# The second round of a fused down projection: each weight sum emitted one unit earlier, and the residual additions spread over more pairs

## Chip, core and metric

The kernel runs on one core of one Trainium2 chip. The metric is device time in microseconds (us) for one execution of the whole program. Five engines work side by side, each on its own in-order list of instructions: TensorE does the matrix products (PE in the profile; PEld is its weight load), VectorE (DVE) and ScalarE (ACT) do elementwise work, GpSimd (POOL) does elementwise work on the side, and SyncE (SP) issues the DMA transfers. [...]

## The reference

A decoder block of sequence 512 and width 1024, in float32. The change touches only the last product, the down projection of the feed-forward part, and the final norm that follows it:

```python
def reference(x, norm_mix_g, w_in, ..., w_ffn_gate, w_ffn_up, w_ffn_down, norm_final_g):
    ...
        h = h + jnp.einsum('bsd,de->bse', merged, w_out[layer])
        u = rmsnorm(h, norm_ffn_g[layer])
        z = (jax.nn.silu(jnp.einsum('bsd,df->bsf', u, w_ffn_gate[layer]))
             * jnp.einsum('bsd,df->bsf', u, w_ffn_up[layer]))
        h = h + jnp.einsum('bsf,fd->bsd', z, w_ffn_down[layer])
    return rmsnorm(h, norm_final_g)
```

`z` is 512x2816 and `w_ffn_down` 2816x1024, so the weight has 22 rows of blocks of 128.

## The kernel before

**High and low parts.** Every product is made of three TensorE products on a faster number format. An operand is split into a high part (a rounded copy) and a low part (what the rounding left): high*high, high*low and low*high are added in PSUM. For a weight, `Weights.split` does this: ScalarE writes the high part `wh` (line 118), then VectorE writes the low part `wl` as weight minus `wh` (line 122). So each weight passes SyncE (load into a tile `raw`), ScalarE, VectorE and TensorE in turn. A unit is one `raw` tile of 128x2048, a quarter of it per product tile; it is split in two halves, the "granules". Names carry the numbers: `raw74` is a unit, `wh149` and `wl149` the parts of its second granule.

**The down projection** is computed by a scheme of fewer block products (as Strassen's): 2x2 blocks of `z` and of the weight are combined by sums and differences, and seven products take the place of eight. It runs in two rounds. The first round uses sums of weight blocks (kind `r1` in `Weights.sums`) and runs between the gate and up projections. The second round, which the change is about, goes over the 11 pairs of weight rows (kind `r2`, units 74 to 84): the even row of a pair needs the sum of its two halves, which VectorE writes in place into the `raw` tile (line 130, `raw<-raw`) before ScalarE can make the high part. A pair gives four products, each 2 row tiles times 3 matmuls of 128x512: `a11b11` and `n1y1` from the even granule, then `a12b21` and `n4b22` from the odd one, 24 matmuls in all. In the profile the PSUM tiles show as `a11b`, `s3y`, `a22y` and `s2y` (the last three are banks taken over from the first round).

**Order.** From the last up projection on, the instructions of VectorE, ScalarE and TensorE keep the order in which the code emits them (`manual_schedule`, the part called `by_hand`). `W.get` hands out the next granule and first splits up to two granules beyond it. `wh` and `wl` have three buffers each, `raw` has two in the old pool and, once the memory of the up projection's input is free, two more (`W.more`). Before the loop over the pairs there is an entry in which the last first-round products, the combination of the last pair's `z` (tile `z8`, lines 1018 to 1029) and the split of unit 74 (`b11h`, `b11l`, `wh149`, `y1h`, `y1l`) interleave. Inside the loop VectorE also adds the first-round products into the residual `hn`, in lump form: four additions behind pair 1, four behind pair 2, and behind pair 3 the last combination of `z` with its split (`zh`, `zl`, lines 1084 to 1086) and the load of the norm's gains. The last three pairs (the tail, units 82 to 84, granules 164 to 169 in the order 164, 166, 165, 167, 168, 169) are split ahead and used by `tail`, product by product, so that finished row tiles can be normalized while others are still multiplied. After `by_hand.close()` the order is a scheduler's.

## Time and profile before

| | |
|---|---|
| median of 3 runs | 903.86 us (902.82 to 904.28) |
| the profiled execution | 904.07 us, span 902.3 us, granted TensorE clock 0.996 |
| busy TensorE | 886.7 us, 98% of the span |
| busy VectorE, ScalarE, GpSimd | 551.4, 396.8 and 154.8 us |
| second round and tail | 827.5 to 894.7 us of the span |

The span is the time from the first to the last instruction that the profiler saw; the execution's own time lies 1.8 us above it. In a timeline row the columns are the start, the length, the engine, the line, the operation, out<-in, the shape and the count; in brackets stands how long the engine had been idle and what ended that. TensorE's matmuls overlap: each row is about 0.39 us long, but at full clock one starts every 0.227 us, so time is counted from start to start. The row of a stretch gives each engine's busy time, then the granted clock of TensorE (1.00 is full), the DMA engines' share and GB/s.

### The profile page before, as it was taken

Reading aid. Unit: us, or ns where it says so; the run is one execution under the profiler, and the core shown is the slowest. Engines: PE = TensorE matmul, PEld = TensorE weight load, DVE = VectorE, ACT = ScalarE, POOL = GpSimd, SP = SyncE. Lnnn points to the kernel's source line nnn. Section 1 sums busy time; section 2 is a strip of 40 time slices with the busy share of each in tenths; the row PEclk is TensorE's granted clock in tenths of the full one; section 3 lists DMA queues with packets and bytes.
Section 4 is the critical chain, followed back from the end, with each engine's and each line's share of the span. In section 5 each row is a group of like instructions: output and inputs, shape, how many; then the busy total and the mean of one; then the engine's idle time right before and its main releaser. Section 6 shows DMA issues by size and latency. Waiting matters only on the chain.

```text
span 902.3 us, 11245 instructions
## 1 busy us (share of the span) xinstructions
PE 886.7 (98%) x4410; PEld 748.0 (83%) x4410; DVE 551.4 (61%) x838; ACT 396.8 (44%) x637; POOL 154.8 (17%) x150
## 2 busy tenths in 40 slices
PE   8999999999999999999999999999999999999986
PEld 7988889888898988888888887888888888887775
DVE  5577877647484755745445345666666556666765
ACT  6566775645363545315333333333333233333444
POOL 3004434300000000000000003332122333320006
PEclk9999999999999999999999999999999999999998
DMA  7231311222212141221434222443434424336522
GB/s 259 94 94 47 94 48 47 94 94 94 94 55 86 48 141 47 94 94 48 140 105 175 61 83 91 139 134 100 140 96 138 139 96 140 125 109 232 208 97 94
DMA packets 74642, 97.26 MB, mean 108 GB/s; under 512 B 2042, under 2 KB 64604, under 8 KB 74588
## 3 DMA queue, kind: packets, MB, share of 16 engines
q1 hardware_dynamic: 74428, 96.27, 32.6%
q8 instruction: 35, 0.57, 0.3%
q10 hardware_dynamic: 160, 0.27, 0.1%
q14 instruction: 19, 0.16, 0.1%
HBM read 94.43 MB, written 2.10 MB: 107 GB/s over the span
## 4 chain that ended last, share of the span: by engine, by line
PE 91%; DVE 3%; ACT 2%; SPq 1%; issue 1%; POOL 0%; DMA 0%; DVEq 0%; POOLq 0%; ACTq 0%
PE ps_big L396 13%; PE ps_big L398 13%; PE ps_big L397 13%; PE ps_f L397 9%; PE ps_f L398 9%; PE ps_f L396 9%; PE s3y L981 2%; PE s2y L981 2%; PE a22y L981 2%; PE ps_v L413 2%; PE ps_v L414 2%; PE ps_v L412 2%; PE ps_o L413 2%; PE ps_o L414 2%; PE ps_o L412 2%; PE pv L538 1%
## 5 line engine op out<-in xcount | busy, mean ns | idle before, releaser
L118 ACT ACTIVATE wh<-raw 128x1024 fp32r<-128x1024 f32 (+1 forms) x168 | 172.1, 1031 | 352.6 <-PE ps_f L397 137.5
L122 DVE TENSOR_TENSOR wl<-raw,wh 128x1024 fp32r<-128x1024 f32 (+1 forms) x168 | 208.4, 1246 | 120.6 <-ACT wh L118 120.4
L396 PE MATMUL ps_big<-uh,wh 128*128 128x512 f32 x376 | 148.8, 396 | 0.0
L397 PE MATMUL ps_big<-ul,wh 128*128 128x512 f32 x376 | 147.8, 393 | 0.0
L398 PE MATMUL ps_big<-uh,wl 128*128 128x512 f32 x376 | 147.7, 393 | 0.0
L397 PE MATMUL ps_f<-u2l,wh 128*128 128x512 f32 x352 | 137.4, 390 | 0.0
L396 PE MATMUL ps_f<-u2h,wh 128*128 128x512 f32 x352 | 137.0, 390 | 0.2 <-ACT u2h L163 0.2
L398 PE MATMUL ps_f<-u2h,wl 128*128 128x512 f32 x352 | 137.0, 389 | 0.0
L398 PEld LDWEIGHTS ps_big<-uh,wl 128*128 128x128 f32 x376 | 70.7, 188 | 14.1
L397 PEld LDWEIGHTS ps_big<-ul,wh 128*128 128x128 f32 x376 | 70.8, 188 | 13.6
L396 PEld LDWEIGHTS ps_big<-uh,wh 128*128 128x128 f32 x376 | 70.7, 188 | 13.5
L396 PEld LDWEIGHTS ps_f<-u2h,wh 128*128 128x128 f32 x352 | 66.0, 188 | 14.2 <-ACT u2h L163 0.5
L398 PEld LDWEIGHTS ps_f<-u2h,wl 128*128 128x128 f32 x352 | 66.1, 188 | 13.9 <-issue 0.2
L397 PEld LDWEIGHTS ps_f<-u2l,wh 128*128 128x128 f32 x352 | 66.1, 188 | 13.7 <-issue 0.2
L946 POOL TENSOR_TENSOR zg<-zg,sgf 128x512 f32<-128x512 f32 x22 | 39.5, 1797 | 190.8 <-ACT sgf L168 190.8
L292 POOL TENSOR_TENSOR r<-ss,neghalf 128x4 f32<-128x4 f32 x8 | 10.1, 1260 | 232.8 <-DVE ss L291 232.8
L130 DVE TENSOR_TENSOR raw<-raw 128x512 f32<-128x512 f32 x44 | 31.9, 724 | 28.6 <-DMA raw<-in_w_ffn_down_dram 28.3
L943 DVE TENSOR_TENSOR zg<-ps_f,R 128x512 f32<-128x512 f32 x22 | 15.1, 691 | 37.9 <-PE ps_f L398 37.9
L947 POOL TENSOR_TENSOR zg<-zg,R 128x512 f32<-128x512 f32 x22 | 37.0, 1683 | 1.7
L412 PE MATMUL ps_v<-wh,uh 128*128 128x256 f32 x128 | 36.5, 285 | 0.0
L413 PE MATMUL ps_v<-wl,uh 128*128 128x256 f32 x128 | 36.3, 284 | 0.0
L414 PE MATMUL ps_v<-wh,ul 128*128 128x256 f32 x128 | 36.2, 284 | 0.0
(328 smaller groups left out, 1615.4 us busy)
## 6 DMA issues: line engine op xcount, KB each, us to landing
raw<-in_w_in_dram SPq DMA_DIRECT2D x27, 1024.0 KB, 5.1
raw<-in_w_ffn_gate_dram SPq DMA_DIRECT2D x11, 1024.0 KB, 5.1
raw<-in_w_ffn_up_dram SPq DMA_DIRECT2D x11, 1024.0 KB, 5.2
raw<-in_w_ffn_down_dram SPq DMA_DIRECT2D x11, 1024.0 KB, 4.8
raw<-in_w_ffn_down_dram SPq DMA_DIRECT2D x22, 512.0 KB, 4.6
raw<-in_w_branch_attn_dram SPq DMA_DIRECT2D x4, 1024.0 KB, 5.5
raw<-in_w_branch_hgrn_dram SPq DMA_DIRECT2D x4, 1024.0 KB, 4.8
raw<-in_w_out_dram SPq DMA_DIRECT2D x4, 1024.0 KB, 5.3
```

The costliest lines, as they stand in the source:

```text
L118: nc.scalar.activation(hv, src, AF.Copy)
L122: (low or nc.vector).tensor_tensor(lv, src, hv.bitcast(F32), ALU.subtract)
L130: add = lambda o, i0, i1: self.nc.vector.tensor_tensor(o, i0, i1, ALU.add)
L396: pe.matmul(ps, wh[:, k, :], ah[:, k, :], start=k == 0, stop=False)
L397: pe.matmul(ps, wh[:, k, :], al[:, k, :], start=False, stop=False)
L398: return raw_ins(pe.matmul(ps, wl[:, k, :], ah[:, k, :], start=False, stop=k == KD - 1))
L412: pe.matmul(ps, ah[:, k0 + k, ts], wh[:, k, :], start=first and k == 0, stop=False)
L413: pe.matmul(ps, ah[:, k0 + k, ts], wl[:, k, :], start=False, stop=False)
L414: pe.matmul(ps, al[:, k0 + k, ts], wh[:, k, :], start=False, stop=last and k == nk - 1)
L946: pool_e.tensor_tensor(zg, zg, sg, ALU.mult)
L947: pool_e.tensor_tensor(zg, zg, R, ALU.mult)
L981: pe.matmul(ps[i], x[:, ts], w, start=first and n == 0, stop=last and n == 2)
```

## The change

Two things. First, the sum of a unit's even row leaves its own split: `sums_ahead` maps a granule to a later granule, and the split of the first emits the sum of the later one between its high and its low part. The map sends each granule of the second round to the one two further on, so the sum of unit u+1 stands ahead of the low part of unit u's even granule; odd rows have no sum, and `summed` keeps any sum from being made twice. The same holds in the tail, and the last sums of the first round (unit 73) move up in the same way. Second, the eight residual additions are spread two per pair over pairs 1 to 4, and the last combination of `z` moves from pair 3 to pair 5 with the release of its pool and the load of the gains.

```diff
@@ split
         if kind in ("r1", "r2"):
-            self.sums(u, half, raw)
+            self.sums(i)
...
             high.tensor_copy(hv, src)
+        if i in self.sums_ahead:
+            self.sums(self.sums_ahead[i])
         with low_after or nullcontext():
             (low or nc.vector).tensor_tensor(lv, src, hv.bitcast(F32), ALU.subtract)
...
-    def sums(self, u, half, raw):
-
-        kind, _, rows = self.units[u]
-        x = [raw[:, 512 * i:512 * i + 512] for i in range(4)]
+    def sums(self, i):
+
+        if i in self.summed or i >= len(self.grans):
+            return
+        self.summed.add(i)
+        u, kind, half = self.grans[i]
+        _, _, rows = self.units[u]
+        x = [self.raw[u][:, 512 * n:512 * n + 512] for n in range(4)]
@@ block_kernel
     r0 = len(W.grans) - NF
+    W.sums_ahead = {r0 - 2: r0 - 1}
...
-    W.sums(W.grans[r0][0], 0, raw)
+    made = list(range(r0 + 1, stream_end + 1))
+    made += [stream_end + 1 + g for g in (0, 2, 1, 3, 4, 5)]
+    W.sums_ahead.update(zip(made[1:], made[3:]))
+    W.sums(r0)
     W.split(r0 + 1)
...
-        if p == 1:
-            for i in range(2):
-                onto(i, 1, s2c[i])
-                tt(evs[i], s2c[i], evs[i], ALU.add)
-        if p == 2:
-            for i in range(2):
-                onto(2 + i, 1, evs[i])
-                onto(2 + i, 0, evs[i], ALU.subtract)
-        if p == 3:
+        if p in (1, 2):
+            onto(p - 1, 1, s2c[p - 1])
+            tt(evs[p - 1], s2c[p - 1], evs[p - 1], ALU.add)
+        if p in (3, 4):
+            onto(p - 1, 1, evs[p - 3])
+            onto(p - 1, 0, evs[p - 3], ALU.subtract)
+        if p == 5:
             tt(n4, a12, s2, ALU.subtract)
             split_form(zh[:, NP - 1], zl[:, NP - 1], z8[:, 0:4, :])
             fp.release()
...
-    for g in (0, 2, 1, 3, 4, 5):
-        if g < 2:
-            W.split(stream_end + 1 + g)
+    for g in made[-2 * TAIL_P:]:
+        if g < stream_end + 3:
+            W.split(g)
         else:
-            W.split(stream_end + 1 + g, wd, 4)
+            W.split(g, wd, 4)
```

TensorE and GpSimd keep their order throughout. On SyncE unit 75 is loaded ahead of unit 76 (it was the other way round), and the load of the gains (`gfin`) moves from between units 82 and 83 to behind unit 84. Three places show what moves on VectorE and ScalarE; the lines after the change lie 2 to 10 further down.

The entry, on VectorE, where the last first-round sums (`raw73`) and the combination of the last `z` stand. Before:

```order
L122 TENSOR_TENSOR wl145_6592<-raw72_6511,wh145_6591 128x1024
L122 TENSOR_TENSOR wl146_6623<-raw73_6585,wh146_6622 128x512
L1018 TENSOR_TENSOR z8_6615<-ps_f_6626,zg_6510 128x2x256
L1019 TENSOR_TENSOR z8_6615<-z8_6615 128x256
L975 TENSOR_TENSOR f1l_6617<-z8_6615,f1h_6616 128x256
L130 TENSOR_TENSOR raw73_6585<-raw73_6585 128x512 x2
L122 TENSOR_TENSOR wl147_6658<-raw73_6585,wh147_6657 128x1024
L975 TENSOR_TENSOR b11l_6687<-raw74_6618,b11h_6686 128x512
L1026 TENSOR_TENSOR z8_6615<-ps_f_6661,zg_6548 128x2x256
```

The same place on VectorE, changed:

```order
L126 TENSOR_TENSOR wl145_6592<-raw72_6511,wh145_6591 128x1024
L138 TENSOR_TENSOR raw73_6585<-raw73_6585 128x512 x2
L126 TENSOR_TENSOR wl146_6623<-raw73_6585,wh146_6622 128x512
L1027 TENSOR_TENSOR z8_6615<-ps_f_6628,zg_6510 128x2x256
L1028 TENSOR_TENSOR z8_6615<-z8_6615 128x256
L983 TENSOR_TENSOR f1l_6617<-z8_6615,f1h_6616 128x256
L126 TENSOR_TENSOR wl147_6658<-raw73_6585,wh147_6657 128x1024
L983 TENSOR_TENSOR b11l_6687<-raw74_6618,b11h_6686 128x512
L1035 TENSOR_TENSOR z8_6615<-ps_f_6661,zg_6548 128x2x256
```

The two sums of unit 73 move from behind the first combination of `z` to ahead of it, past `wl146`.

The loop, on VectorE, from the low parts of unit 76 (pair 2) on. `s2c`, `z8` and `ev` hold first-round products. Before:

```order
L122 TENSOR_TENSOR wl152_6789<-raw76_6734,wh152_6788 128x1024
L122 TENSOR_TENSOR wl153_6805<-raw76_6734,wh153_6804 128x1024
L1048 TENSOR_TENSOR hn_4420<-hn_4420,s2c_6751 128x512
L1078 TENSOR_TENSOR ev_6701<-s2c_6751,ev_6701 128x512
L1048 TENSOR_TENSOR hn_4420<-hn_4420,z8_6615 128x512
L1078 TENSOR_TENSOR ev_6702<-z8_6615,ev_6702 128x512
L130 TENSOR_TENSOR raw77_6737<-raw77_6737 128x512
L122 TENSOR_TENSOR wl154_6829<-raw77_6737,wh154_6828 128x1024
L122 TENSOR_TENSOR wl155_6845<-raw77_6737,wh155_6844 128x1024
L1048 TENSOR_TENSOR hn_4420<-hn_4420,ev_6701 128x512 x2
L1048 TENSOR_TENSOR hn_4420<-hn_4420,ev_6702 128x512 x2
L130 TENSOR_TENSOR raw78_6754<-raw78_6754 128x512
```

The same place on VectorE, changed:

```order
L126 TENSOR_TENSOR wl152_6789<-raw76_6734,wh152_6788 128x1024
L126 TENSOR_TENSOR wl153_6806<-raw76_6734,wh153_6805 128x1024
L1057 TENSOR_TENSOR hn_4420<-hn_4420,s2c_6751 128x512
L1089 TENSOR_TENSOR ev_6701<-s2c_6751,ev_6701 128x512
L138 TENSOR_TENSOR raw78_6754<-raw78_6754 128x512
L126 TENSOR_TENSOR wl154_6827<-raw77_6737,wh154_6826 128x1024
L126 TENSOR_TENSOR wl155_6844<-raw77_6737,wh155_6843 128x1024
L1057 TENSOR_TENSOR hn_4420<-hn_4420,z8_6615 128x512
L1089 TENSOR_TENSOR ev_6702<-z8_6615,ev_6702 128x512
L138 TENSOR_TENSOR raw79_6785<-raw79_6785 128x512
L126 TENSOR_TENSOR wl156_6865<-raw78_6754,wh156_6864 128x1024
L126 TENSOR_TENSOR wl157_6882<-raw78_6754,wh157_6881 128x1024
```

Ahead of a unit's low parts now stands the sum of the next unit, and two additions instead of four lie between units.

The tail, on VectorE, from the last granule of unit 81 on. Before:

```order
L122 TENSOR_TENSOR wl163_7005<-raw81_6864,wh163_7004 128x1024
L130 TENSOR_TENSOR raw82_6912<-raw82_6912 128x512
L122 TENSOR_TENSOR wl164_7046<-raw82_6912,wh164_7045 128x1024
L130 TENSOR_TENSOR raw83_6948<-raw83_6948 128x512
L122 TENSOR_TENSOR wl166_7051<-raw83_6948,wh166_7050 128x1024
L130 TENSOR_TENSOR raw82_6912<-raw82_6912 128x512
L122 TENSOR_TENSOR wl165_7056<-raw82_6912,wh165_7055 128x1024
L122 TENSOR_TENSOR wl167_7060<-raw83_6948,wh167_7059 128x1024
```

The same place on VectorE, changed (the first sum of `raw82` and that of `raw83` now stand further up, ahead of `wl162` and of `wl163`):

```order
L126 TENSOR_TENSOR wl163_7006<-raw81_6861,wh163_7005 128x1024
L138 TENSOR_TENSOR raw82_6899<-raw82_6899 128x512
L126 TENSOR_TENSOR wl164_7047<-raw82_6899,wh164_7046 128x1024
L126 TENSOR_TENSOR wl166_7052<-raw83_6937,wh166_7051 128x1024
L126 TENSOR_TENSOR wl165_7056<-raw82_6899,wh165_7055 128x1024
L126 TENSOR_TENSOR wl167_7060<-raw83_6937,wh167_7059 128x1024
```

No sum is left between the low parts of granules 164, 166 and 165.

At the very end of the tail, on ScalarE, where the last squares for the norm (`jkd`) and the scaling of the last row tiles (`hn`) stand. Before:

```order
L163 ACTIVATE jkd_7186,s2d_7081<-hn_4420 128x512
L163 ACTIVATE jkd_7208,s2d_7104<-hn_4420 128x512
L163 ACTIVATE jkd_7220,s2d_7104<-hn_4420 128x256
L163 ACTIVATE jkd_7223,s2d_7104<-hn_4420 128x256
L163 ACTIVATE hn_4420<-hn_4420,r1d_7192 128x512
L163 ACTIVATE hn_4420<-hn_4420,r1d_7229 128x512
```

The same place on ScalarE, changed:

```order
L171 ACTIVATE jkd_7186,s2d_7081<-hn_4420 128x512
L171 ACTIVATE jkd_7208,s2d_7104<-hn_4420 128x512
L171 ACTIVATE jkd_7220,s2d_7104<-hn_4420 128x256
L171 ACTIVATE hn_4420<-hn_4420,r1d_7192 128x512
L171 ACTIVATE jkd_7223,s2d_7104<-hn_4420 128x256
L171 ACTIVATE hn_4420<-hn_4420,r1d_7229 128x512
```

The scaling of row tile 0 (`r1d_7192`) now stands between the two last squares of row tile 1. The code of this part is not edited; the scheduler chose this order.

## Prediction

> **What bounds the kernel now.** I read the page's busy shares first (TensorE 98%), then who made TensorE wait in the second round and tail, then its timeline around each wait. The list of waits from 780 us on names four places (engine, waiting line, releaser, total, times, longest):

> ```profile
> PE a11b L981 <- DVE wl L122: 1.5, 2, 0.8
> PE a11b L1109 <- ACT wh L118: 1.5, 1, 1.5
> PE a11b L1109 <- DVE wl L122: 0.8, 1, 0.8
> PE s3y L981 <- DVE y1l L975: 0.5, 1, 0.5
> ```

> That is 4.3 us of waits, but they cost more, as the starts of the matmuls show:

> ```profile
> 827.49 0.40 PE L981 MATMUL s2y<-wh,f1l 128*128 128x512 f32 x1
> ...
> 829.04 0.50 PE L981 MATMUL s3y<-y1l,zh 128*128 128x512 f32 x1 [0.51 <-DVE y1l L975]
> ...
> 830.31 0.39 PE L981 MATMUL a22y<-wh,zh 128*128 128x512 f32 x1
> ...
> 849.47 0.42 PE L981 MATMUL a11b<-wh,zh 128*128 128x512 f32 x1
> ...
> 856.30 0.50 PE L981 MATMUL a11b<-wh,zh 128*128 128x512 f32 x1
> ...
> 862.89 0.39 PE L981 MATMUL a11b<-wh,zh 128*128 128x512 f32 x1
> ...
> 873.77 0.39 PE L1109 MATMUL a11b<-wh,zh 128*128 128x512 f32 x1
> ...
> 876.11 0.50 PE L1109 MATMUL a11b<-wh,zh 128*128 128x512 f32 x1 [1.49 <-ACT wh L118]
> 877.36 0.67 PE L1109 MATMUL a11b<-wl,zh 128*128 128x512 f32 x1 [0.76 <-DVE wl L122]
> ...
> 881.11 0.39 PE L1109 MATMUL a11b<-wl,zh 128*128 128x512 f32 x1
> ...
> 894.30 0.39 PE L1109 MATMUL s2y<-wh,zl 128*128 128x512 f32 x1
> ```

> 862.89 and 873.77 are the first matmuls of unit 80 and of the tail, two units or 48 matmuls apart: 10.88 / 48 = 0.2267 us each, with no wait. By this rate each stretch has a loss:
> - 827.49 to 830.31, 7 matmuls: 2.82 against 1.59, loss 1.23.
> - 830.31 to 849.47, 84 matmuls: 19.16 against 19.04, loss 0.12.
> - 849.47 to 862.89 (units 78 and 79), 48 matmuls: 13.42 against 10.88, loss 2.54.
> - 873.77 to 894.30, 71 matmuls: 20.53 against 16.10, loss 4.43.

> Together 8.3 us is what an unbroken TensorE would save. In the last term sits a slow stretch behind the two waits:

> ```profile
> 877.36:881.11 3.75, 3.75 (x9) 2.94 (x10) 3.75 (x4) 2.13 (x3) 0.66 (x1) 0.54 0.00 0
> ```

> The granted clock is 0.54 there; 9 matmuls took 3.75 instead of 2.04, so 1.7 of the 4.43 is clock, the other 2.7 the waits.

> **The change part by part.** It adds and removes no instruction; it moves 11 VectorE sums, 8 additions, one combination with its split, and two loads.

> *The loop, the 2.54.* Before, VectorE and ScalarE took turns, shown by two units of VectorE and one of ScalarE:

> ```profile
> 840.78 0.69 DVE L130 TENSOR_TENSOR raw<-raw 128x512 f32<-128x512 f32 x1
> 842.74 2.36 DVE L122 TENSOR_TENSOR wl<-raw,wh 128x1024 fp32r<-128x1024 f32 x2 [1.26 <-ACT wh L118]
> 845.01 2.49 DVE L1048 TENSOR_TENSOR hn<-hn,ev 128x512 f32<-128x512 f32 x4
> 847.42 0.69 DVE L130 TENSOR_TENSOR raw<-raw 128x512 f32<-128x512 f32 x1
> 841.64 2.01 ACT L118 ACTIVATE wh<-raw 128x1024 fp32r<-128x1024 f32 x2 [4.47 <-DVE raw L130]
> ```

> From sum to sum 6.64 us: sum, 1.26 idle for `wh`, two low parts, four additions. TensorE eats a unit in 24 x 0.2267 = 5.44, so it caught up and waited. Afterwards `wh` no longer depends on a sum that VectorE has just made: sum 0.6 + low parts 2.3 + two additions 1.2 = 4.1 us a unit, 1.3 less than TensorE needs. ScalarE needs 2.0. What paces both is then the three buffers. One is free 0.47 us after the start of its last matmul:

> ```profile
> 865.39 0.39 PE L981 MATMUL s3y<-wh,zl 128*128 128x512 f32 x1
> 865.86 1.06 ACT L118 ACTIVATE wh<-raw 128x1024 fp32r<-128x1024 f32 x1 [1.16 <-PE s3y L981]
> ```

> With T the start of the unit before, the next unit's even `wh` starts when that unit's predecessor is read out, T + 0.24, and ends at 1.3; its low part ends by 2.5, or 3.7 with both additions and a sum in front; it is needed at T + 5.67. Unit 81 is the tightest: behind unit 80's start come the split of `z` and unit 82's sum on VectorE, so that `wl162` ends at 4.2, still 1.4 early. I take all of 2.54 and 0.1 of the 0.12. Bounds: nothing, if buffers rather than VectorE caused the waits, and 2.66. The value is nearer the top because of that 1.4.

> *The entry, the 1.23.* VectorE:

> ```profile
> 817.00 0.69 DVE L1018 TENSOR_TENSOR z<-ps_f,zg 128x512 f32<-128x512 f32 x1 [2.92 <-PE ps_f L398]
> 818.98 1.41 DVE L130 TENSOR_TENSOR raw<-raw 128x512 f32<-128x512 f32 x2
> 821.59 1.22 DVE L122 TENSOR_TENSOR wl<-raw,wh 128x1024 fp32r<-128x1024 f32 x1 [1.21 <-ACT wh L118]
> 822.74 0.68 DVE L975 TENSOR_TENSOR b11l<-raw,b11h 128x512 fp32r<-128x512 f32 x1
> 823.34 0.68 DVE L1026 TENSOR_TENSOR z<-ps_f,zg 128x512 f32<-128x512 f32 x1
> 821.94 0.39 PE L398 MATMUL ps_f<-u2h,wl 128*128 128x512 f32 x1
> 828.30 0.69 DVE L975 TENSOR_TENSOR y1l<-raw,y1h 128x512 fp32r<-128x512 f32 x1
> ```

> The two sums (1.41) move into the 2.92 us in which VectorE idled ahead of 817.00; without that cover they would delay the combination by 1.4. Then `wh147` and `wl147` come some 2 us earlier, `b11l` too, and the second combination, which stood at 823.34 behind them, waits only for its product: last matmul 821.94 plus 0.50 gives 822.44, 0.9 earlier. From there VectorE and ScalarE are one chain to `y1l`, which ends at 828.1 instead of 829.0. TensorE wants it at 827.49 + 2 x 0.2267 = 827.94, waits 0.2 and loses 0.1 restarting: 0.35 stays, 0.9 goes (bounds 0, if another input of the chain is late, and 1.23).

> *The tail, the 4.43.* The loop that ran dry, VectorE and ScalarE:

> ```profile
> 874.14 0.68 DVE L130 TENSOR_TENSOR raw<-raw 128x512 f32<-128x512 f32 x1
> 876.08 4.63 DVE L122 TENSOR_TENSOR wl<-raw,wh 128x1024 fp32r<-128x1024 f32 x4 [1.26 <-ACT wh L118]
> 875.00 3.90 ACT L118 ACTIVATE wh<-raw 128x1024 fp32r<-128x1024 f32 x4 [2.03 <-DVE raw L130]
> ```

> Sum, `wh165`, `wl165` in a row, 874.14 to 877.3, released TensorE at 877.36. With the sums done before, `wh165` starts when its buffer (that of `wh162`) is free. With T the start of unit 81 that is T + 2.49 + 0.47 = 2.96; `wh165` ends at 4.0, `wl165` at 5.2; needed at T + 24 x 0.2267 + 0.68 = 6.1. So no wait, 0.9 to spare, and with nothing idle the clock stays up: 4.43 goes (bounds 0 and 4.43; the value has the margin on its side).

> *The end.* ScalarE now scales row tile 0 before the last square:

> ```profile
> 895.78 0.42 ACT L163 ACTIVATE jkd<-hn 128x256 f32<-128x256 f32 x1
> 896.20 0.71 ACT L163 ACTIVATE hn<-hn,r1d 128x512 f32<-128x512 f32 x1
> 896.50 0.14 DVE L1143 TENSOR_REDUCE s1d<-s2d 128x1 f32<-128x5 f32 x1
> 897.13 0.55 POOL L1145 TENSOR_TENSOR r1d<-s1d,neghalf 128x1 f32<-128x1 f32 x1
> ```

> The reduction behind that square slips by about 0.6, to 897.1 (in the old clock); GpSimd took it up at 897.13, having been busy until then, and now would at about 897.4. Cost 0.25 (bounds 0 and 0.7).

> *Loads.* SyncE issues unit 75 as soon as `wl147` is done, unit 76 when the projection's memory is free (as before), and the gains last, behind the last low part of unit 80: on the reckoning above at about 862.5. They are first used by GpSimd in the tail,

> ```profile
> 884.39 5.08 POOL L1141 TENSOR_TENSOR hn<-hn,gfin 128x512 f32<-128x512 f32 x4
> ```

> or 7.7 us earlier, 14 us behind their issue. The sum of unit 76, now 1.2 us of idle VectorE time ahead of `wl150`, stands at 829.8. In the summary of the tile `raw`, landing takes

> ```profile
> DMA to landing us min/median/max: 3.6/4.6/6.6
> ```

> From issues at about 822.4 that is 829.0 at the worst: cost 0, bounds 0 and 0.5.

> Sum: 0.9 + 0.1 + 2.5 + 4.4 - 0.25 = 7.7 us. The profiled execution, 904.07, becomes 896.4; it stood 0.2 above the median, so the median becomes 903.86 - 7.7 = 896.2, with 1 us to either side from the bounds of entry and end.

> **Rivals.**
> - *The slow clock stays.* Were the stretch at 0.54 not the work of the waits ahead of it, 1.7 would stay: 897.9. Against: behind a single wait of 0.8 us the clock is 1.00, and only here do two follow at once (1.49 and 0.76):

> ```profile
> 850.60:853.00 2.40, 2.35 (x10) 1.94 (x11) 1.47 (x2) 0.90 (x1) 0.00 (x0) 1.00 0.18 27
> ```

>   [...]
> - *The tail's wait stays.* If the buffers hold up `wh165` (the 865.86 row shows ScalarE already waiting for one), 4.4 is not won and 3.3 is: 900.6. Against: the 0.9 to spare.
> - *Nothing but the entry.* If buffers also pace the loop, only 0.65 comes: 903.2, no change to measure. Against: the row at 865.86 is the first such wait in the loop; in units 76 to 79 ScalarE waited for VectorE's sum.
> - *Slower: sums waiting for loads.* A sum ahead of the low parts holds them if its unit has not landed. In the loop the sum comes 10.4 us after the issue (the unit four back ends its low parts, 828.1; the sum of unit 78 at 838.5), and 2.7 us lie between low part and use. From a landing of 13 us TensorE waits; it ends slower when that passes 1.1 us in each of seven units, a landing of 14.2, twice the longest above.

> **How the numbers follow.** The forecast 0.74; the slow clock 0.08; the tail's wait 0.08; nothing but the entry 0.05; slower 0.03; 0.02 for gains in between. The range 895.0 to 899.0 holds the forecast with its 1 us and the slow clock, 0.8. Faster by over 0.2% (1.8 us, about what a measurement tells from no change): 0.92; within 0.05; slower 0.03.

> **What would show it.** Right: no wait of TensorE behind 829 us, none on `wl` or `wh` in the loop; matmuls 0.227 apart through the tail, clock 1.00; VectorE idle for TensorE's buffers rather than for ScalarE; the wait for `y1l` near 0.2. Wrong: a wait at the second granule of the tail, a stretch at half clock, or VectorE idle for a load ahead of a sum.

## The result and the profile after

The changed kernel takes 895.86 us (median of 6 runs, 895.52 to 896.35); the kernel before, run beside it, 903.81 us (6 runs, 902.82 to 904.28). The ratio is 0.9914, with a 95% interval of 0.9902 to 0.9927. The prediction said 896.2, with a range of 895.0 to 899.0. The profiled execution took 895.81 us, its span is 894.1 us, the granted TensorE clock 0.998.

The list of TensorE's waits from 780 us on (engine, waiting line, releaser, total, times, longest) had four rows before; one is left:

```profile
PE s3y L989 <- DVE y1l L983: 0.2, 1, 0.2
```

The timeline of TensorE at the places that the prediction counts from, in the changed kernel: the entry, the first `a22y` behind it, a hitch, the first matmuls of unit 78 (848.27) and of the tail (870.03), and the last matmul:

```profile
827.07 0.39 PE L989 MATMUL s2y<-wh,f1l 128*128 128x512 f32 x1
...
827.84 0.50 PE L989 MATMUL s3y<-y1l,zh 128*128 128x512 f32 x1 [0.15 <-DVE y1l L983]
...
829.10 0.39 PE L989 MATMUL a22y<-wh,zh 128*128 128x512 f32 x1
...
832.07 0.47 PE L989 MATMUL a11b<-wl,zh 128*128 128x512 f32 x1
832.38 0.39 PE L989 MATMUL a11b<-wh,zl 128*128 128x512 f32 x1
...
848.27 0.39 PE L989 MATMUL a11b<-wh,zh 128*128 128x512 f32 x1
...
870.03 0.39 PE L1119 MATMUL a11b<-wh,zh 128*128 128x512 f32 x1
...
886.13 0.39 PE L1119 MATMUL s2y<-wh,zl 128*128 128x512 f32 x1
```

Measured against the unbroken rate of 0.2267 us a matmul, as the prediction did:

| stretch | matmuls | took | unbroken | loss now | loss before |
|---|---|---|---|---|---|
| 827.07 to 829.10 | 7 | 2.03 | 1.59 | 0.44 | 1.23 |
| 829.10 to 848.27 | 84 | 19.17 | 19.04 | 0.13 | 0.12 |
| 848.27 to 870.03 | 96 | 21.76 | 21.76 | 0.0 | 2.54 |
| 870.03 to 886.13 | 71 | 16.10 | 16.10 | 0.0 | 4.43 |

So TensorE won 0.79 + 2.54 + 4.43 - 0.01 = 7.75 us here. Its last matmul comes 8.17 us earlier (894.30 against 886.13), because the changed kernel's trace already stood 0.42 earlier at the first of these rows; 0.31 of that is there at the first combination of `z` (817.00 against 816.69). Executions differ by that much anyway: in three profiles of the kernel before (the one above and the two repeats at the end of the experiments) the first of these rows stands at 827.49, 826.96 and 827.15. The 0.42 is therefore not counted as a gain of the change. The span fell by 8.2, the median by 7.95.

The stretch at half clock is gone as well. A stretch of the tail in the changed kernel (busy time of PE, PEld, DVE, ACT, POOL with counts, granted clock, DMA share, GB/s) has the clock at 1.00; 13 matmuls start in the 3 us, the row's 15 counts every one that reaches into them.

```profile
873.00:876.00 3.00, 3.00 (x15) 2.49 (x14) 3.00 (x6) 1.21 (x3) 2.45 (x2) 1.00 0.00 0
```

The timeline of VectorE at the entry, changed kernel:

```profile
813.10 1.40 DVE L138 TENSOR_TENSOR raw<-raw 128x512 f32<-128x512 f32 x2
...
816.69 0.69 DVE L1027 TENSOR_TENSOR z<-ps_f,zg 128x512 f32<-128x512 f32 x1 [1.59 <-PE ps_f L406]
...
822.13 0.69 DVE L1035 TENSOR_TENSOR z<-ps_f,zg 128x512 f32<-128x512 f32 x1 [1.03 <-PE ps_f L406]
...
827.10 0.68 DVE L983 TENSOR_TENSOR y1l<-raw,y1h 128x512 fp32r<-128x512 f32 x1
```

The two sums of unit 73 (813.10) now lie in what was 2.92 us of idle time ahead of 816.69, of which 1.59 is left. The second combination no longer stands behind other work: VectorE is idle for 1.03 us until its product comes.

The timeline of VectorE and ScalarE over one unit in the loop, changed kernel:

```profile
843.75 0.68 DVE L138 TENSOR_TENSOR raw<-raw 128x512 f32<-128x512 f32 x1
844.36 1.22 DVE L126 TENSOR_TENSOR wl<-raw,wh 128x1024 fp32r<-128x1024 f32 x1
846.85 1.23 DVE L126 TENSOR_TENSOR wl<-raw,wh 128x1024 fp32r<-128x1024 f32 x1 [1.27 <-ACT wh L120]
847.99 1.28 DVE L1057 TENSOR_TENSOR hn<-hn,ev 128x512 f32<-128x512 f32 x2
849.19 0.69 DVE L138 TENSOR_TENSOR raw<-raw 128x512 f32<-128x512 f32 x1
...
843.08 1.06 ACT L120 ACTIVATE wh<-raw 128x1024 fp32r<-128x1024 f32 x1 [1.71 <-PE s2y L989]
845.75 1.06 ACT L120 ACTIVATE wh<-raw 128x1024 fp32r<-128x1024 f32 x1 [1.61 <-PE s3y L989]
```

From sum to sum it is 5.44 us (843.75 to 849.19), TensorE's own pace, where it was 6.64. VectorE still shows 1.27 us of waiting for `wh`, and the row names ScalarE, as before. But ScalarE, which then waited 4.47 us for VectorE's sum, now waits for TensorE to read a buffer out (1.71 and 1.61). That is how one tells a loop in which two engines hold each other up from one that is paced by its consumer: the releaser of the releaser.

### The profile page after: what moved, and what is told of

It reads as the page before. It is cut to its first block, busy times and chain, and to the rows that moved or that the text cites. A ratio compares the mean times of both kernels' runs of the same rounds, so it can differ in the third digit from the quotient of the medians.

```text
span 894.1 us, 11244 instructions
## 1 busy us (share of the span) xinstructions
PE 882.6 (99%) x4410; PEld 746.8 (84%) x4410; DVE 551.3 (62%) x838; ACT 397.0 (44%) x637; POOL 155.1 (17%) x150
## 4 chain that ended last, share of the span: by engine, by line
PE 96%; SPq 1%; DVE 1%; ACT 1%; POOL 0%; issue 0%; DMA 0%; DVEq 0%; POOLq 0%; ACTq 0%
PE ps_big L404 13%; PE ps_big L405 13%; PE ps_big L406 13%; PE ps_f L405 9%; PE ps_f L406 9%; PE ps_f L404 9%; PE s3y L989 3%; PE a22y L989 3%; PE s2y L989 3%; PE ps_v L421 2%; PE ps_v L422 2%; PE ps_v L420 2%; PE ps_o L421 2%; PE ps_o L422 2%; PE ps_o L420 2%; PE pv L546 1%
## 5 line engine op out<-in xcount | busy, mean ns | idle before, releaser
L406 PEld LDWEIGHTS ps_big<-uh,wl 128*128 128x128 f32 x376 | 70.7, 188 | 14.2
```

What stands on the lines that cost most here:

```text
L406: return raw_ins(pe.matmul(ps, wl[:, k, :], ah[:, k, :], start=False, stop=k == KD - 1))
```

## The experiments

The theory: TensorE lost time because VectorE's sum, ScalarE's high part and VectorE's low part followed each other within one granule; the sums ahead break that chain, and this, not the spreading, is the gain. Rivals: the additions in lumps of four made VectorE late; the tail alone makes the gain; the half clock is a matter of its own. The times are medians, each beside the kernel before in the same comparison.

**Spreading alone.** Additions two per pair as in the changed kernel, no sum moved:

```diff
-    W.sums_ahead = {r0 - 2: r0 - 1}
+    W.sums_ahead = {}
...
-    W.sums_ahead.update(zip(made[1:], made[3:]))
```

> The kernel before with the additions spread, and no sum moved. My theory (VectorE's alternation with ScalarE costs 6.6 us a unit only where four additions stand in it; with two it is 0.6 + 1.26 + 2.3 + 1.2 = 5.35, just under TensorE's 5.44): the waits in units 78 and 79 go (2.5 us), but the split of z now falls on unit 80 and puts the tail's granules about 1 us later, so that the tail loses 4.4 to 5.4: 902.0, 901.3 at the best, half clock still there. Rival (only moved sums help): 903.8 and the waits of units 78 and 79 stay.

903.24 against 903.52 us, ratio 1.0001 (0.9992 to 1.0011): no change, and 1.2 us more than expected. TensorE's waits from 826 us on, the last two rows of four left out:

```profile
PE a11b L1118 <- ACT wh L120: 2.8, 1, 2.8
PE a11b L1118 <- DVE wl L126: 0.8, 1, 0.8
```

The two waits of the loop are gone, so fewer additions in a row do cure the loop. But the first wait of the tail has grown from 1.49 to 2.8. TensorE starts the tail 2.6 us earlier (871.16 against 873.77); VectorE is not as much earlier, for there the sum and the low part still alternate with ScalarE. VectorE in the tail, this kernel:

```profile
869.90 0.68 DVE L138 TENSOR_TENSOR raw<-raw 128x512 f32<-128x512 f32 x1
871.71 1.22 DVE L126 TENSOR_TENSOR wl<-raw,wh 128x1024 fp32r<-128x1024 f32 x1 [1.13 <-ACT wh L120]
872.86 0.68 DVE L138 TENSOR_TENSOR raw<-raw 128x512 f32<-128x512 f32 x1
874.80 4.63 DVE L126 TENSOR_TENSOR wl<-raw,wh 128x1024 fp32r<-128x1024 f32 x4 [1.26 <-ACT wh L120]
```

The last of these sums stands at 872.86, against 874.14 before: 1.3 earlier, where TensorE came 2.6 earlier. The other 1.3 went into the longer wait, and behind it the clock stayed at half for longer (two stretches of TensorE's clock, this kernel):

```profile
876.00:879.00 3.00, 2.92 (x7) 2.34 (x8) 3.00 (x4) 1.99 (x3) 0.00 (x0) 0.50 0.00 0
879.00:882.00 3.00, 3.00 (x9) 2.32 (x8) 2.23 (x4) 0.94 (x3) 1.87 (x2) 0.50 0.00 0
```

The last matmul comes at 894.20, before it was 894.30. From 871.16 on the tail's 71 matmuls lost 6.94 us, where 5.4 at most was expected. What the loop won, the tail lost.

**Sums alone.** The sums ahead, the additions in lumps of four again:

```diff
-        if p in (1, 2):
-            onto(p - 1, 1, s2c[p - 1])
-            tt(evs[p - 1], s2c[p - 1], evs[p - 1], ALU.add)
...
+        if p == 1:
+            for i in range(2):
+                onto(i, 1, s2c[i])
+                tt(evs[i], s2c[i], evs[i], ALU.add)
...
```

> The changed kernel with the additions in lumps of four again and the combination of z behind pair 3. My theory (once the sums are ahead, VectorE needs at most 0.6 + 2.3 + 2.4 = 5.3 us for a unit against 5.44): all of the gain stays, 895.9 within 0.3, no wait in the loop; the spread is then worth nothing by itself. Rival (the lumps are what holds the low parts): the 2.5 us of units 78 and 79 come back in part, 897 to 898.4.

895.83 against 903.52 us, ratio 0.9918 (0.9902 to 0.9935). That is the whole gain; the 0.2 us for `y1l` is the only wait of TensorE. Once the sums stand ahead, the spreading adds nothing to measure.

**The tail's sums alone.** Lumps, and only the sums of the tail ahead:

```diff
-    W.sums_ahead = {r0 - 2: r0 - 1}
+    W.sums_ahead = {}
...
-    W.sums_ahead.update(zip(made[1:], made[3:]))
+    W.sums_ahead.update((g, h) for g, h in zip(made[1:], made[3:]) if h > stream_end)
...
```

> The kernel before with only the three sums of the tail (units 82 and 83) moved ahead; entry, loop and additions as before. My theory: the 4.4 us of the tail go, waits and slow clock together, and the rest stays: 899.4, granted clock 1.00 throughout the tail. Rival (the slow clock is not the work of the waits): the waits of 2.7 go, the half-clock stretch of 1.7 stays: 901.1.

899.58 against 903.52 us, ratio 0.9962 (0.9949 to 0.9975): 3.9 us from the tail. The loop's waits (1.5 us) and the full wait for `y1l` (0.5) stay, the tail has none, and its last matmul is at 890.33.

**All but the tail's sums.**

```diff
-    W.sums_ahead.update(zip(made[1:], made[3:]))
+    W.sums_ahead.update((g, h) for g, h in zip(made[1:], made[3:]) if h <= stream_end)
```

> The changed kernel with the three sums of the tail back in their own splits. My theory: the loop and the entry keep their 3.5 us, the tail loses its 4.4 again (two waits of 1.5 and 0.8 us, then some 3.4 us at half clock): 900.3. Since the split of z now falls on unit 80, up to 0.5 more. Rival (in the changed kernel TensorE reaches the tail earlier relative to its loads, so that the tail would stall by another cause and the sums are not it): 896.

901.15 against 903.52 us, ratio 0.9975 (0.9965 to 0.9984), 0.9 slower than expected. The waits of the tail are back to the size they had before, TensorE's list:

```profile
PE a11b L1119 <- ACT wh L120: 1.5, 1, 1.5
PE a11b L1119 <- DVE wl L126: 0.8, 1, 0.8
```

and yet the clock behind them (the waits end at 873.8) is whole:

```profile
873.00:876.00 3.00, 2.24 (x11) 1.82 (x11) 3.00 (x4) 2.86 (x4) 0.06 (x1) 1.00 0.00 0
```

The tail (870.22 to 889.12) lost 2.80 us at TensorE and not the 4.43 expected. TensorE is done at 889.12, 5.2 us earlier than before, but the span is only 2.9 shorter. The end behind the last matmul took 10.3 us in place of 8.0: the scheduler, which orders that part by itself, gave ScalarE's squares and scalings another order, and VectorE's reduction stood waiting for one of them. VectorE's timeline:

```profile
889.44 0.16 DVE L1153 TENSOR_REDUCE s1d<-s2d 128x1 f32<-128x5 f32 x1 [3.29 <-ACT jkd L171]
```

An edit far ahead of the end thus moved the end by 2.3 us. Where an experiment does that, its time doesn't tell what its edit was worth; TensorE's starts, up to the last matmul, do.

**One sum of the tail ahead**, that of unit 83, beside the loop's:

```diff
-    W.sums_ahead.update(zip(made[1:], made[3:]))
+    W.sums_ahead.update((g, h) for g, h in zip(made[1:], made[3:])
+                        if h <= stream_end or h == stream_end + 3)
```

> The changed kernel, but of the tail's three sums only that of unit 83 stays ahead; both sums of unit 82 are back in their own splits. One hand-over less in the tail: TensorE should wait once, about 0.8 us, for the low part of granule 165, with no wait for its high part. If the half clock comes from the two waits in a row (2.25 us of idle), it stays at 1.00 here: 0.9 lost, 896.8. If any wait in the tail starts it: another 1.7, 898.5.

897.46 against 903.72 us, ratio 0.9931 (0.9916 to 0.9947). One wait of 0.8 us for `wl` is left in the tail, the clock stays at 1.00, as forecast for a single wait. But the tail (870.40 to 887.69) lost 1.2 us at TensorE where 0.9 was expected: the wait is listed with 0.77, but from the matmul ahead of it to the one behind it 1.26 us pass (871.11 to 872.37) in place of 0.23. In the time it is 1.6 against the changed kernel.

**Entry alone.** Lumps, and only unit 73's sums ahead (its entry in `sums_ahead` kept, the others left out):

```diff
     W.sums_ahead = {r0 - 2: r0 - 1}
...
-    W.sums_ahead.update(zip(made[1:], made[3:]))
...
```

> The kernel before with only the two sums of unit 73 moved ahead; loop, additions and tail as before. My theory: the entry's 0.9 us are gained there (the wait for y1l falls from 0.5 to 0.2), TensorE reaches the loop 0.9 earlier, but VectorE, which paces units 75 to 79, also starts 0.9 earlier, so that the gain is kept: 902.9. Rival (the loop takes it back, since TensorE only waits longer for VectorE in unit 78): 903.8.

903.48 against 904.13 us, ratio 0.9996 (0.9987 to 1.0005): no gain in time. TensorE did win: the seven matmuls from 827.22 to 829.25 lost 0.44 us, as in the changed kernel, and not 1.23; the wait for `y1l` is 0.2. The loop did not take it back: units 78 and 79 took 13.41 us (848.43 to 861.84), 13.42 before. But the end went the same way as above, 10.35 us behind the last matmul (891.65):

```profile
891.96 0.16 DVE L1154 TENSOR_REDUCE s1d<-s2d 128x1 f32<-128x5 f32 x1 [3.27 <-ACT jkd L171]
```

So the time of this run decides nothing about the entry; TensorE's rows speak for the forecast and against its rival.

**Further ahead.** If one unit is good, are two better? The sum of each unit's even row two units ahead, then, for units 78 to 81, three ahead (the text of the second expectation names the units otherwise than the edit has them; the edit holds):

```diff
-    W.sums_ahead.update(zip(made[1:], made[3:]))
+    W.sums_ahead.update(zip(made[1:], made[5:]))
```

> The changed kernel with each sum two units ahead instead of one. The sum then stands about 5 us behind its load's issue instead of 10.4, against a landing of 4.5 (3.5 to 6.4): VectorE waits for loads by up to 1.4 us, which its margin ahead of TensorE (1.4 to 2.7 us) covers. My theory: the same time, 895.9 within 0.5, no wait of TensorE in the loop. Rival (loads are already the edge): each unit waits, 898 or more.

```diff
-    W.sums_ahead.update(zip(made[1:], made[3:]))
+    W.sums_ahead.update((g, h) for g, h in zip(made[1:], made[7:]) if h <= stream_end)
+    W.sums_ahead.update((g, h) for g, h in zip(made[1:], made[3:]) if h > stream_end)
```

> The changed kernel with the sums of units 79, 80 and 81 three units ahead (units 76 and 77 then make their own; the tail as in the changed kernel). A sum now stands directly behind the low part that frees its buffer, so it waits a whole landing, 4.5 us, and holds the low parts behind it. My theory (the rival of the prediction in which sums wait for loads, brought about): TensorE waits about 2 us in each of units 76, 77 and 78, 6.3 together, 902.2; if single waits of 2 us also halve the clock, up to 5 more, 907. Rival (loads are hidden anyway): 896.

Two units: 896.51 against 903.72 us, ratio 0.9921 (0.9908 to 0.9935). Three: 903.24 against 903.72, ratio 0.9997 (0.9988 to 1.0006): the whole gain gone. They are 0.6 and 1.0 slower than expected. VectorE's timeline with two units ahead:

```profile
830.48 0.69 DVE L138 TENSOR_TENSOR raw<-raw 128x512 f32<-128x512 f32 x1 [1.16 <-DMA raw<-in_w_ffn_down_dram]
```

and with three, VectorE and TensorE:

```profile
833.87 0.69 DVE L138 TENSOR_TENSOR raw<-raw 128x512 f32<-128x512 f32 x1 [4.02 <-DMA raw<-in_w_ffn_down_dram]
...
835.75 0.80 PE L989 MATMUL a11b<-wl,zh 128*128 128x512 f32 x1 [3.27 <-DVE wl L126]
```

The sum stands in VectorE's list ahead of a low part that could have run, and holds it until its load has landed (1.16 and 4.02 us in these rows). That is the prediction's last rival, and its mechanism is real; one unit ahead just doesn't reach it. At two units it costs a wait of 0.4 us, where none was expected; at three 3.27 us and half clock behind it (0.50 from 837 to 839), and two more waits of 0.8 and 1.0.

**What stays of the entry.** Making `y1l` before `wl149`. The new function `split_y1` takes the tiles `y1h` and `y1l` and calls `split_form` for them; granule 149's split calls it between its high and its low part:

```diff
+        if i in self.between:
+            self.between[i]()
         if i in self.sums_ahead:
...
+    W.between = {r0 + 1: split_y1}
     W.split(r0 + 1)
-    split_form(y1h, y1l, raw[:, 512:1024])
```

> The changed kernel, and in the entry the split of y1 stands between the high and the low part of granule 149, so that y1l comes 0.6 to 1.1 us earlier than wl149. My theory: the last wait (0.15 us for y1l, 0.4 with the restart) goes and none takes its place: 895.5, 0.4 less than the changed kernel. Rival (the chain through y1h, which waits for its sum, is what is late): no change, 895.9.

896.70 against 903.72 us, ratio 0.9923 (0.9911 to 0.9936): the wait for `y1l` is gone, and 0.8 was lost against the changed kernel where 0.4 was to be won. TensorE's waits:

```profile
PE a11b L992 <- DVE wl L129: 0.4, 1, 0.4
PE a22y L992 <- DVE hn L1060: 0.3, 1, 0.3
```

Against TensorE's matmuls `y1l` came only 0.3 earlier, not 0.6 to 1.1, because VectorE waited 0.78 us for `y1h` ahead of it; that much of the rival holds. `wl149`, the two residual additions and the sum of unit 75 then followed, the last two 0.85 us later against TensorE than in the changed kernel. So the next to be late were the PSUM bank that the additions read out (`a22y` at 829.59) and the first low part of unit 75, `wl150` (`a11b<-wl` at 833.19).

The next version therefore also puts unit 74's sum into the idle time ahead of the second combination, and the two additions ahead of `y1l`:

```diff
     split_form(b11h, b11l, raw[:, 0:512])
+    W.sums(r0)
...
     def split_y1():
+        for i in range(2):
+            onto(2 + i, 0, banks["a22y4"][i])
```

> The changed kernel with VectorE's entry in another order: the sum of unit 74 up ahead of the second combination of z, into 1.0 us of idle time, then the two additions that free the first-round banks, then y1l, and only then wl149. My theory (the 0.4 us lost at y1l is only a matter of order, and the one before failed because the additions and unit 75's sum came too late): both the wait for y1l and the hitch at unit 75 go, no wait is left behind 827 us, last matmul 0.4 earlier: 895.4. Rival (VectorE has no time left in the entry): a wait at granule 149 or 150 takes its place, 895.9 or more.

895.12 us (895.0 to 895.67, 5 runs) against 903.73, ratio 0.9911 (0.9897 to 0.9924). TensorE's list of waits from 826 us on is empty. VectorE and TensorE in this kernel:

```profile
820.92 0.69 DVE L141 TENSOR_TENSOR raw<-raw 128x512 f32<-128x512 f32 x1
822.03 0.69 DVE L1039 TENSOR_TENSOR z<-ps_f,zg 128x512 f32<-128x512 f32 x1 [0.42 <-PE ps_f L409]
...
825.36 1.37 DVE L1061 TENSOR_TENSOR hn<-hn,a22y 128x512 f32<-128x512 f32 x2
826.64 0.69 DVE L986 TENSOR_TENSOR y1l<-raw,y1h 128x512 fp32r<-128x512 f32 x1
...
826.97 0.39 PE L992 MATMUL s2y<-wh,f1l 128*128 128x512 f32 x1
827.20 0.39 PE L992 MATMUL s3y<-y1h,zh 128*128 128x512 f32 x1
827.43 0.46 PE L992 MATMUL s3y<-y1l,zh 128*128 128x512 f32 x1
827.72 0.39 PE L992 MATMUL s3y<-y1h,zl 128*128 128x512 f32 x1
...
828.65 0.40 PE L992 MATMUL a22y<-wh,zh 128*128 128x512 f32 x1
...
885.63 0.39 PE L1128 MATMUL s2y<-wh,zl 128*128 128x512 f32 x1
```

The sum at 820.92 fills the idle second ahead of the combination (0.42 is left), `y1l` starts 0.46 earlier than in the changed kernel, and the matmul that had waited starts 0.23 behind its forerunner. The last matmul comes 0.5 earlier than in the changed kernel; 0.1 of that is there at the first of TensorE's rows (826.97 against 827.07), so 0.4 is won, as forecast. It is the lowest median of all versions. But the two were not timed beside each other: the ranges (895.0 to 895.67 and 895.52 to 896.35) overlap a little, and by their ratios to the kernel before (0.9911 and 0.9914) the times can't be told apart.

**The half clock.** The kernel before once more, twice, each with its profile:

> The kernel before once more, unchanged, for the granted clock behind the tail's two waits (1.5 and 0.8 us). If the waits by themselves bring half clock: a stretch at 0.54 again, last matmul 8 us from the end of the span at about 894.3. [...]

> The same once more: with two waits of 1.5 and 0.8 us, half clock or not, as in the run before this one.

They took 902.42 and 903.6 us. Both have the same waits at the same places (1.5 and 0.8 in the tail). The stretch behind them in the first, and in the second:

```profile
877.00:881.00 4.00, 4.00 (x18) 3.27 (x19) 4.00 (x5) 2.53 (x4) 2.00 (x1) 1.00 0.00 0
```

```profile
877.00:881.00 4.00, 3.98 (x11) 3.16 (x12) 4.00 (x5) 2.15 (x3) 0.86 (x1) 0.57 0.00 0
```

18 matmuls reach into the 4 us in one and 11 in the other, with one program. The first was done with its matmuls at 892.21, the second at 893.94. Of these 1.73 us, 0.17 is there at the tail's first matmul (873.25 and 873.42); the rest, 1.56, is what the stretch cost at TensorE. In the time it is 1.2.

What decides between the two outcomes is in the traces. The granted clock changes only on a grid of 3.413 us: half clock lasted 3.41 us in the first profile of the kernel before, in the second repeat and with three units ahead, and 6.83, twice as long, with the spreading alone; the full clock between two changes lasted 17.07 (5 steps) or 870.40 us (255 steps) in that first profile. Where the grid lies against the program differs from run to run: its first edge behind the tail's first matmul comes 0.34 us after it in the first profile, 1.92 in the first repeat and 0.32 in the second. So the waits by themselves do not bring half clock; it hangs on where the grid falls as well. The step that holds the waits, in the second repeat and in the first:

```profile
873.74:877.15 3.41, 1.16 (x5) 0.42 (x4) 2.15 (x4) 2.50 (x3) 0.00 (x0) 1.00 0.00 0
```

```profile
875.17:878.58 3.41, 2.24 (x8) 1.61 (x9) 3.02 (x3) 3.41 (x5) 0.00 (x0) 1.00 0.00 0
```

In the second repeat both waits fall into one step, TensorE is idle for 2.25 of its 3.41 us, and the next step (877.15 to 880.56) runs at half clock (0.50); the first profile of the kernel before has the same (2.25, from 874.11 on). In the first repeat an edge of the grid cuts the first wait, and the two steps have 1.08 and 1.17 us idle. With the entry alone they have 0.66 and 1.59, with all but the tail's sums 1.50 and 0.76, and the clock behind them is 1.00 in these three. Laid over all 14 profiles, every step at full clock with 2.25 us idle or more is followed by half clock (those behind the last matmul among them), and none with 1.85 us (the last version of the entry, 884.45 to 887.87) or less.

The mean granted clock on record for each run is a hint at how often this happens. Of the 59 runs of the kernel before beside the experiments, 17 have 0.997 or 0.998 and took 902.33 to 903.0 us; 42 have 0.996 or less and took 903.29 us or more. The three profiles of this kernel fit that (0.996, 0.997 and 0.996, half clock in the first and the last). It is a hint only, because the mean also holds the half clock behind the last matmul (0.50 from 898.01 us on in the first profile): the entry alone has 0.996 with no half clock ahead of that.

## Why the prediction was right

The time was 0.3 below the forecast, and the mechanism was the one forecast. From profiled execution to profiled execution it is 8.26 us (904.07 to 895.81) where 7.7 were forecast: 7.75 by TensorE's losses, 0.42 because it started earlier, 0.03 at the end, the small rest outside. The 0.42 is luck: nothing forecast it, and executions of one program differ by as much. By its steps:

- **The loop, 2.54 forecast, 2.54 measured.** The two waits are gone, VectorE needs 5.44 - 1.27 = 4.17 us of a unit where 4.1 was reckoned, and ScalarE now waits for buffers. The 0.1 beside it did not come: a loss of 0.13 stays, most of it at the hitch between 832.07 and 832.38. VectorE, ScalarE and TensorE's weight load there, changed kernel:

```profile
828.90 1.29 DVE L138 TENSOR_TENSOR raw<-raw 128x512 f32<-128x512 f32 x2
829.66 2.01 ACT L120 ACTIVATE wh<-raw 128x1024 fp32r<-128x1024 f32 x2 [1.42 <-issue]
830.76 2.36 DVE L126 TENSOR_TENSOR wl<-raw,wh 128x1024 fp32r<-128x1024 f32 x2 [0.57 <-ACT wh L120]
832.04 0.19 PEld L989 LDWEIGHTS a11b<-wl,zh 128*128 128x128 f32 x1 [0.23 <-DVE wl L126]
```

  Unit 75 is the one unit of the loop whose sum isn't moved: the map starts at its own granule 150 (`made[1:]`), so no earlier split emits its sum, and sum, high part and low part still follow each other. Its low part ends at 831.98 and the weight load behind it comes just too late. The kernel before has the same late load (833.24), and so has the kernel with the spreading alone. What the prediction did not see is that the loop was cured twice over: either part alone clears its waits.
- **The tail, 4.43 forecast, 4.43 measured**, in TensorE's rows. `wh165` and `wl165` were never late. In the changed kernel's timeline the last four of the tail's six high parts run as a block from 867.56, `wh165` first, and their low parts from 868.66, ahead of the tail's first matmul at 870.03. With T = 864.59 for the start of unit 81 (859.15 + 5.44), `wh165` starts at T + 2.97, where 2.96 was reckoned. The experiments with the tail's sums in, out, and one of them, show that the sums do it: 3.9 us of time alone, both waits back without them, one wait with one of them.
- **The half clock in it, 1.7.** The prediction laid it to the two waits. They were needed for it, but it came only where the grid of 3.413 us left both in one step: with waits of 1.49 and 0.76 us it came in two profiles (the one before and one repeat) and failed to come in three (the other repeat, all but the tail's sums, entry alone). Its size, 1.7 in the prediction, is 1.56 at TensorE and 1.2 in the time by the two repeats; the waits with their restarts are the larger part, 2.86 in the repeat without it (873.25 to 892.21). The prediction took the half clock from one execution as if it were in each. That the tail's sum came out to the hundredth is therefore partly luck: the profile it was read from had the half clock, as most runs seem to.
- **The entry, 0.9 forecast, 0.79 measured.** The second combination stands at 822.13, 0.31 ahead of the 822.44 forecast, just the shift of the whole trace; the wait for `y1l` is 0.15 where 0.2 was said. The mis-sized term is what stays behind it: 0.44 where 0.35 was said. In the version without the wait the same seven matmuls took 1.68 (826.97 to 828.65), a loss of 0.09, so waiting and restarting made up 0.35 of the 0.44.
- **The end, 0.25 forecast, nothing measured.** It did get the other order, and the reduction slipped, by 0.3 and not by 0.6. VectorE and GpSimd at the end, changed kernel:

```profile
888.62 0.16 DVE L1153 TENSOR_REDUCE s1d<-s2d 128x1 f32<-128x5 f32 x1 [0.17 <-ACT jkd L171]
...
886.90 2.13 POOL L1151 TENSOR_TENSOR hn<-hn,gfin 128x512 f32<-128x512 f32 x2
889.00 0.55 POOL L1155 TENSOR_TENSOR r1d<-s1d,neghalf 128x1 f32<-128x1 f32 x1
```

  The reduction comes 2.49 us behind the last matmul (2.20 before), but GpSimd was busy until 889.03 anyway, and `r1d` starts 2.87 behind it where it was 2.83. The slip was covered by GpSimd; the prediction left 0.25 uncovered.
- **The loads, 0 forecast.** The gains were issued at 861.7 (about 862.5 forecast), and no sum waits for a load. The experiments with two and three units ahead bound how much room there was: one unit more already has VectorE waiting 1.16 us.
- **The rivals.** The slow clock did not stay once the waits were gone. The wait of the tail did not stay, and neither did the loop's. Nothing here speaks for buffers as the cause: VectorE, ScalarE and TensorE had the same three buffers throughout.

Not settled: in how many of the runs the half clock came, for only three executions of the kernel before have a trace, and what a step with between 1.85 and 2.25 us of idle time brings.

## What to carry to other kernels

Where two engines make a consumer's operand in turn (A, B, then A again) with in-order lists, look at the releaser of the releaser; if A and B wait for each other, moving A's first step one unit ahead takes B's latency out of the loop, though only as far ahead as its load has landed, since a step that waits for its load holds what stands behind it (1.16 us with two units ahead, 4.02 with three). A cure in the loop can be worth nothing if the tail behind it has the same chain: with the spreading alone TensorE merely arrived there earlier and waited longer. With the sums ahead in the loop VectorE was earlier too, and the tail's waits kept their size. So change both and count the gain at the last matmul. And read an experiment at the engine that is the bound as well as by its time, because a scheduler can reorder an end that the edit doesn't touch (2.3 us here).
